# A one-core transformer layer: squares and the sine product on VectorE, softmax rows in pairs, a float32r spread of the norm's factor, and a final norm written in place

## The chip, the cores and the metric

The program runs on one core of a Trainium2 chip. Five engines work on it, each through a queue of its own that it takes strictly in order: TensorE (PE, with its weight loads PEld), VectorE (DVE), ScalarE (ACT), GpSimd (POOL) and SyncE (SP, which here only issues DMAs). The metric is the device time of one execution in microseconds (us), as a median over runs.

## The reference, cut to what matters

One layer on x of 1024 tokens by 1024 channels, everything in float32:

```python
hn = rmsnorm(h, norm_mix)                       # x / sqrt(mean(x*x) + eps) * gain
qa, ka, va, qb, kb, vb = split(hn @ w_in)       # 8 heads / 2 kv heads, and 8 heads, of 64
qa, ka = partial_rope(qa), partial_rope(ka)     # [x1*cos - x2*sin, x2*cos + x1*sin, rest]
o_a = window attention, |i-j| <= 128, with a sink logit in each softmax row
o_b = 2-D neighbourhood attention, 8 x 16 window, with a bias
h = h + concat(rmsnorm(o_a), rmsnorm(o_b)) @ w_out
h = h + (silu(conv(hn @ w_gate) + b) * (hn @ w_up)) @ w_down      # hn = rmsnorm(h, norm_ffn)
return rmsnorm(h, norm_final)
```

## The kernel before, in words

Tensors lie transposed, channels on the 128 partitions and the 1024 tokens along the row, so x is eight tiles of 128x1024. A float32 product is made of three float32r matmuls, high by high, high by low and low by high: each operand is split into a rounded part (`hi`, cast by ACT) and the rest (`lo`, subtracted by DVE). `block` (lines 112 to 115) and `group` (783 to 787) issue the three, each 128x128 by 128x512. PE takes its instructions in the order of the program text (line 91). DVE, ACT, POOL and SP are put in order by a scheduler at build time, from priorities and its own estimate of when things are ready; what it decided is a fixed row of instructions on each engine.

**Start and first norm.** For each of the eight tiles of x, ACT writes `xgh` (line 125) and DVE `xgl` (126), and PE multiplies them at once with the first two weight tiles (`first`, banks `pj` and `o`); the norm's factor is applied only afterwards. Beside it `squares` (135 to 143) squares the tiles on ACT (`sq`, 139) and adds them up, tile after tile, on the engine that its caller names (141): POOL for the first norm (560), DVE for the norm of group A later on. `inverse_narrow` (145) sums the squares over the partitions: 128x1 matmuls with `ones` give a 128x4 column block `ss`, ACT takes the root (153), DVE the reciprocal (154). `widen` (157) spreads that `v` over all partitions again: four float32 matmuls of each 128-column against the identity in `cst` (161), each of which the trace counts as two rows. ACT copies the result into `rstd` (574). This is done for the token halves h = 0 and 1; then `evacuate` (168, line 170) multiplies the banks `pj`, `o` and `s` (third weight tile) with `rstd` on DVE.

**Projections and attention.** Sixteen more projections follow, mixed with attention as filler. `rotate` (178 to 185) applies the rotary part to a tile `t` of heads: two small DMAs fetch the partner channels into `u`, DVE makes t*rc (183), POOL u*rs (184), DVE adds (185). `split_pair` (188) then scales and splits the tile into the operands `q` (190, 192) and moves halves by DMA. Scores (266) come into banks `s`; `softmax` (277 to 290) runs per row block j: POOL copies the sink logit beside it (283), DVE adds the mask and takes the row maximum in one custom instruction (284, with a small read of the result `nm`), ACT the exponential with its sum `sm` (288), DVE the reciprocal of `sm` (289), POOL scales the block (290). Two blocks share a tile `p`; PE transposes them (322, 395), ACT and DVE split the result (`ph`, `pl`, 295 and 296), PE multiplies by v (327, 328).

**Feed-forward and end.** The gated feed-forward runs as matrix products p1 to p7 over blocks, then the down-projection (banks `dn`, order written out at 1049 to 1057) as seven products p. `leave` (1202) adds each finished 128x512 bank to the residual (`add`, 1176) and squares it (`square`, 1180; DVE adds to the running sum at 1185). When p = 6 has begun, the token half h = 1 is complete: `inverse_narrow` for it at (j, c) = (0, 2) and `finish` at (1, 2), while PE goes on with `dn`. The half h = 0 is finished after the last matmul (1245). `finish` (1188) widens v, lets ACT copy the bank into `wide` (1191), and makes eight output tiles: for d = 2 and 5 ACT scales the residual (1196) and POOL multiplies by the copy (1197), for the other six DVE does both in one instruction that reads the bank (1199). They go to `y` tiles, of a pool tag with six buffers, and SP sends them out in the order of d (1200).

## Time and profile before

| | |
|---|---|
| median of 3 runs | 1141.33 us (1141.04 to 1143.16) |
| profiled execution: time / span | 1136.96 / 1135.0 us |
| PE busy / mean granted clock | 1088.1 us (96% of the span) / 0.986 |
| DVE, ACT, POOL busy | 874.7, 550.2, 149.1 us |
| chain that ended last | PE 82%, DVE 8%, DMA 3%, issue 3%, ACT 2%, POOL 1% |

The rows of the timeline view read: start, duration, engine, line, operation, output tile <- input tiles, shape, count, and in brackets the idle time of that engine before it with what ended it. Rows of several like instructions are joined (x4). A window row gives, for a stretch of time, its length and then the busy time (and count) of PE, PEld, DVE, ACT and POOL, the granted PE clock, the busy share of the DMA engines and GB/s. A matmul row lasts longer than the step to the next one, since they are pipelined: at full clock one 128x512 matmul starts 0.23 us after the one before it.

### The profile page before, as it was taken

The numbers are of one execution on the slowest core, as the hardware profiler recorded it, in microseconds if no ns is written. First come the engines' busy times: TensorE is split into PE (matmuls) and PEld (weight loads), VectorE is DVE, ScalarE is ACT, GpSimd is POOL, SyncE is SP. The second block draws the span as 40 slices with busy tenths as digits, with TensorE's granted clock in tenths as the row PEclk, the third lists the DMA queues.
The fourth block names the chain that finished last, engine by engine and source line by source line (L and its number), as shares of the span: only waits on it lengthen the run. The fifth ranks groups of instructions, "written<-read, shape, count | busy, mean of one in ns | idle before, by whom it ended". The sixth has DMA issues, their size and how long they took to land.

```text
span 1135.0 us, 15044 instructions
## 1 busy us (share of the span) xinstructions
PE 1088.1 (96%) x5124; PEld 903.0 (80%) x5124; DVE 874.7 (77%) x1594; ACT 550.2 (48%) x1033; POOL 149.1 (13%) x233
## 2 busy tenths in 40 slices
PE   7989999999999989999899999999999899999995
PEld 5867788888878878888688888888888688888884
DVE  6687888766689667899988778877887778886843
ACT  6235677655767534445443334333433554543531
POOL 4634533233223100000000000000000000000001
PEclk8999999999999999999999999999999999999998
DMA  7242120233305317402542223222322799775723
GB/s 273 72 119 74 48 57 28 73 95 89 78 28 150 101 47 241 146 31 96 192 131 103 107 89 129 94 103 93 123 101 93 232 319 298 260 226 163 261 78 148
DMA packets 65294, 147.17 MB, mean 130 GB/s; under 512 B 7969, under 2 KB 14113, under 8 KB 65217
## 3 DMA queue, kind: packets, MB, share of 16 engines
q1 hardware_dynamic: 56256, 121.17, 34.1%
q10 hardware_dynamic: 8960, 25.04, 5.8%
q8 instruction: 40, 0.66, 0.2%
q14 instruction: 38, 0.30, 0.1%
HBM read 104.37 MB, written 28.57 MB: 117 GB/s over the span
## 4 chain that ended last, share of the span: by engine, by line
PE 82%; DVE 8%; DMA 3%; issue 3%; ACT 2%; POOL 1%; SPq 0%; POOLq 0%; ACTq 0%; DVEq 0%
PE dn L785 6%; PE dn L786 6%; PE dn L787 6%; PE pj L113 6%; PE pj L114 6%; PE pj L115 6%; PE z L785 5%; PE z L787 5%; PE z L786 5%; PE x L785 3%; PE x L786 3%; PE x L787 3%; PE y L787 3%; PE y L785 3%; PE y L786 3%; PE s L266 3%
## 5 line engine op out<-in xcount | busy, mean ns | idle before, releaser
L774 ACT ACTIVATE whi<-ws 128x512 fp32r<-128x512 f32 (+1 forms) x100 | 60.1, 623 | 125.4 <-DVE ws L891 85.5
L785 PE MATMUL dn<-xd,whi 128*128 128x512 f32 x308 | 120.0, 390 | 0.0
L787 PE MATMUL dn<-xd,wlo 128*128 128x512 f32 x308 | 119.8, 389 | 0.0
L786 PE MATMUL dn<-xd,whi 128*128 128x512 f32 x308 | 119.8, 389 | 0.0
L785 PE MATMUL z<-hg,whi 128*128 128x512 f32 x264 | 103.4, 392 | 2.4 <-DVE gs L941 2.4
L787 PE MATMUL z<-hg,wlo 128*128 128x512 f32 x264 | 103.7, 393 | 0.2 <-DVE wlo L775 0.2
L113 PE MATMUL pj<-xgh,whi 128*128 128x512 f32 x248 | 103.8, 418 | 0.0
L786 PE MATMUL z<-hg,whi 128*128 128x512 f32 x264 | 103.3, 391 | 0.0
L290 POOL TENSOR_SCALAR p<-p,sm 128x384 f32<-128x384 f32 (+1 forms) x128 | 77.4, 606 | 192.1 <-DVE sm L289 165.3
L1197 POOL TENSOR_TENSOR y<-y,wide 128x512 f32<-128x512 f32 x4 | 5.1, 1280 | 734.1 <-ACT y L1196 734.1
L288 ACT ACTIVATE p<-p,nm 128x385 f32<-128x385 f32 (+3 forms) x128 | 74.9, 586 | 49.4 <-DVE nm L284 43.9
L114 PE MATMUL pj<-xgl,whi 128*128 128x512 f32 x248 | 97.8, 394 | 0.3 <-DVE xgl L126 0.3
L115 PE MATMUL pj<-xgh,wlo 128*128 128x512 f32 x248 | 98.1, 396 | 0.0
L775 DVE TENSOR_TENSOR wlo<-raw,whi 128x512 fp32r<-128x512 f32 (+1 forms) x102 | 66.5, 671 | 22.1 <-ACT whi L774 21.1
L774 ACT ACTIVATE whi<-raw 128x512 fp32r<-128x512 f32 (+1 forms) x102 | 61.0, 612 | 46.3 <-DMA raw<-in_w_down_dram 11.1
L775 DVE TENSOR_TENSOR wlo<-ws,whi 128x512 fp32r<-128x512 f32 (+1 forms) x100 | 66.9, 681 | 19.8 <-ACT whi L774 19.7
L296 DVE TENSOR_TENSOR pl<-pt,ph 128x384 fp32r<-128x384 f32 (+2 forms) x108 | 63.2, 588 | 21.5 <-ACT ph L295 20.2
L295 ACT ACTIVATE ph<-pt 128x384 fp32r<-128x384 f32 (+2 forms) x108 | 55.3, 514 | 40.6 <-PE pt L395 29.4
L1098 ACT ACTIVATE xd<-xd 128x512 fp32r<-128x512 f32 x77 | 46.9, 626 | 54.1 <-DMA xd<-x 50.7
L787 PE MATMUL y<-hg,wlo 128*128 128x512 f32 x176 | 69.4, 394 | 2.2 <-DVE wlo L775 2.2
L785 PE MATMUL y<-hg,whi 128*128 128x512 f32 x176 | 69.1, 393 | 1.9 <-ACT whi L774 1.9
L785 PE MATMUL x<-hg,whi 128*128 128x512 f32 x176 | 68.8, 391 | 1.4 <-ACT c L925 1.4
(201 smaller groups left out, 2721.9 us busy)
## 6 DMA issues: line engine op xcount, KB each, us to landing
xd<-x SPq DMA_DIRECT2D x77, 256.0 KB, 4.9
raw<-in_w_down_dram SPq DMA_DIRECT2D x72, 256.0 KB, 3.5
raw<-in_w_gate_dram SPq DMA_DIRECT2D x22, 512.0 KB, 3.4
raw<-in_w_up_dram SPq DMA_DIRECT2D x22, 512.0 KB, 5.6
x<-c ACTq DMA_DIRECT2D x22, 512.0 KB, 2.9
raw<-in_w_in_dram SPq DMA_DIRECT2D x32, 256.0 KB, 2.7
raw<-in_w_down_dram SPq DMA_DIRECT2D x36, 192.0 KB, 3.9
x<-t ACTq DMA_DIRECT2D x11, 512.0 KB
```

Source lines behind the costliest of these rows:

```text
L113: nc.tensor.matmul(ps, w[0], x[0][:, tsl(h)], start=first, stop=False)
L114: nc.tensor.matmul(ps, w[0], x[1][:, tsl(h)], start=False, stop=False)
L115: nc.tensor.matmul(ps, w[1], x[0][:, tsl(h)], start=False, stop=last)
L288: nc.scalar.activation(p[:, j, 0:e], p[:, j, 0:e], AF.Exp, bias=nm, scale=-1.0, accum_out=sm)
L290: nc.gpsimd.tensor_scalar(p[:, j, 0:n], p[:, j, 0:n], sm, 1.0, op0=ALU.mult, op1=ALU.mult)
L295: nc.scalar.activation(ph[:, 0:n], ps[:, 0:n], AF.Copy)
L296: nc.vector.tensor_tensor(pl[:, 0:n], ps[:, 0:n], f32(ph[:, 0:n]), op=ALU.subtract)
L774: nc.scalar.activation(hi, src, AF.Copy)
L775: nc.vector.tensor_tensor(lo, src, f32(hi[:, :, :]), op=ALU.subtract)
L785: nc.tensor.matmul(ps, w[0], x[0], start=first and i == 0, stop=False, skip_group_check=True)
L786: nc.tensor.matmul(ps, w[0], x[1], start=False, stop=False, skip_group_check=True)
L787: nc.tensor.matmul(ps, w[1], x[0], start=False, stop=last and i == len(ws) - 1, skip_group_check=True)
```

## The change

Six things change.

1. **Squares:** the first norm's sum of squares is added up by DVE, not POOL.
2. **Sine product:** u*rs of `rotate` moves from POOL to DVE.
3. **Softmax in pairs:** the two blocks of a tile share a 128x2 `sm`; one reciprocal and both POOL scalings follow when the second block is there, and one copy brings both sinks.
4. **Spread in float32r:** `inverse_narrow` splits the factor on DVE (a cast to `v4h`, a subtraction to `v4l`), and `widen` sends both, eight single-pass matmuls against a float32r identity instead of four float32 ones. The sums over partitions run operand by operand, no longer column by column. `ones` shrinks to a column.
5. **End of the final norm:** `finish` widens twice, into one bank for DVE and one for ACT's copy; the outputs are written over the residual tiles, with no `y`; for d = 2 and 5 ACT scales the residual ahead of time (`scaled`, at p = 6), so that only POOL's product remains.
6. **Last tile:** its addition and square go in two halves of 256 columns.

```diff
-        ones = cpool.tile([128, 128], F32, name="ones")
+        ones = cpool.tile([128, 1], F32, name="ones")
...
+        ident_r = cpool.tile([128, 128], F32R, name="ident_r")
...
         def inverse_narrow(sqs, dim, tag):
             ps = bank("ss", tag)
-            for c in range(4):
-                for i, sq in enumerate(sqs):
+            for i, sq in enumerate(sqs):
+                for c in range(4):
                     nc.tensor.matmul(ps[:, c:c + 1], sq[:, c * 128:(c + 1) * 128], ones[:, 0:1], start=c == 0 and i == 0,
                                      stop=i == len(sqs) - 1, skip_group_check=True)
             v = cpool.tile([128, 4], F32, name="v4", tag="v4", bufs=4)
+            hi, lo = (cpool.tile([128, 4], F32R, name=n, tag=n, bufs=4) for n in ("v4h", "v4l"))
             nc.scalar.activation(v, ps[:, 0:4], AF.Sqrt, bias=eps, scale=float(D) / dim)
             nc.vector.reciprocal(v, v)
-            return v
+            nc.vector.tensor_copy(hi, v)
+            nc.vector.tensor_tensor(lo, v, f32(hi[:, :]), op=ALU.subtract)
+            return hi, lo
...
             for c in range(4):
-                nc.tensor.matmul(wide[:, c * 128:(c + 1) * 128], v[:, c:c + 1].to_broadcast([128, 128]), ident, start=True, stop=True)
+                for i, part in enumerate(v):
+                    nc.tensor.matmul(wide[:, c * 128:(c + 1) * 128], part[:, c:c + 1].to_broadcast([128, 128]), ident_r,
+                                     start=c == 0 and i == 0, stop=i == 1, skip_group_check=True)
...
-            nc.gpsimd.tensor_tensor(u[0:n], u[0:n], rs[0:n], op=ALU.mult)
+            nc.vector.tensor_tensor(u[0:n], u[0:n], rs[0:n], op=ALU.mult)
...
-        def softmax(p, j, ps, n, bias, nsink=None):
+        def softmax(st, j, ps, n, bias, nsink=None):
...
+                if j == 0:
+                    st["sm"], st["n"] = spool.tile([128, 2], F32, name="sm"), [n, n]
+                sm, st["n"][j] = st["sm"], n
+                if nsink is not None and j == 0:
+                    nc.gpsimd.tensor_copy(p[:, 0:2, n:n + 1], nsink.rearrange("p (j o) -> p j o", o=1))
...
-                nc.vector.reciprocal(sm, sm)
-                nc.gpsimd.tensor_scalar(p[:, j, 0:n], p[:, j, 0:n], sm, 1.0, op0=ALU.mult, op1=ALU.mult)
+                if j == 1:
+                    nc.vector.reciprocal(sm, sm)
+                    for i, m in enumerate(st["n"]):
+                        nc.gpsimd.tensor_scalar(p[:, i, 0:m], p[:, i, 0:m], sm[:, i:i + 1], 1.0, op0=ALU.mult, op1=ALU.mult)
...
+        nc.gpsimd.tensor_copy(ident_r, ident)
...
-        acc = squares(xts, nc.gpsimd)
+        acc = squares(xts, nc.vector)
...
         def finish(h, v, tag):
             wide = widen(v, tag)
             copy = half("wide")
-            nc.scalar.activation(copy, wide, AF.Copy)
+            nc.scalar.activation(copy, widen(v, tag), AF.Copy)
             for d in range(KT):
-                y = half("y")
                 x = res[d][:, tsl(h)]
-                if d % 3 == 2:
-                    nc.scalar.activation(y, x, AF.Copy, scale=col(C_NFIN + d))
-                    nc.gpsimd.tensor_tensor(y, y, copy, op=ALU.mult)
+                if d in (2, 5):
+                    nc.gpsimd.tensor_tensor(x, x, copy, op=ALU.mult)
                 else:
-                    nc.vector.scalar_tensor_tensor(y, x, col(C_NFIN + d), wide, op0=ALU.mult, op1=ALU.mult)
-                nc.sync.dma_start(out[d, :, tsl(h)], y)
+                    nc.vector.scalar_tensor_tensor(x, x, col(C_NFIN + d), wide, op0=ALU.mult, op1=ALU.mult)
+                nc.sync.dma_start(out[d, :, tsl(h)], x)
+        def scaled(d, h):
+            x = res[d][:, tsl(h)]
+            nc.scalar.activation(x, x, AF.Copy, scale=col(C_NFIN + d))
...
+                if (d, h) == (KT - 1, 0):
+                    s2 = half("s2")
+                    for cols in (slice(0, 256), slice(256, HALF)):
+                        add(d, h, ps, cols)
+                        nc.scalar.activation(s2[:, cols], res[d][:, cols], AF.Square)
+                    sq[h] = [sq[h], s2]
+                    return
...
+            if p == 6 and (j, c) in ((0, 1), (3, 1)):
+                for d in (2, 5):
+                    scaled(d, 1 if j == 0 else 0)
```

How the rows on the engines move is shown at three places. The first is VectorE's row at the start, from the second tile of x to the weight parts `wlo` that follow the first norm. Before:

```order
L126 SCALAR_TENSOR_TENSOR xgl<-xt,par,xgh 128x1024 x2
L109 TENSOR_TENSOR wlo<-raw,whi 128x512
L126 SCALAR_TENSOR_TENSOR xgl<-xt,par,xgh 128x1024 x3
L109 TENSOR_TENSOR wlo<-raw,whi 128x512
L126 SCALAR_TENSOR_TENSOR xgl<-xt,par,xgh 128x1024 x2
L542 TENSOR_SCALAR nsink<-par 128x8
L566 TENSOR_TENSOR wlo_314<-raw_312,whi_313 128x1024
```

and with the change (L127 is the old L126, L142 the old L141, L110 the old L109):

```order
L127 SCALAR_TENSOR_TENSOR xgl<-xt,par,xgh 128x1024
L142 TENSOR_TENSOR sq<-sq 128x1024
L127 SCALAR_TENSOR_TENSOR xgl<-xt,par,xgh 128x1024
L110 TENSOR_TENSOR wlo<-raw,whi 128x512
L142 TENSOR_TENSOR sq<-sq 128x1024
L127 SCALAR_TENSOR_TENSOR xgl<-xt,par,xgh 128x1024
L142 TENSOR_TENSOR sq<-sq 128x1024
L127 SCALAR_TENSOR_TENSOR xgl<-xt,par,xgh 128x1024 x2
L110 TENSOR_TENSOR wlo<-raw,whi 128x512
L127 SCALAR_TENSOR_TENSOR xgl<-xt,par,xgh 128x1024
L142 TENSOR_TENSOR sq<-sq 128x1024
L556 TENSOR_SCALAR nsink<-par 128x8
```

The seven additions of squares now stand between the `xgl`; three of them ahead of the fourth `xgl`, and the last three behind the seventh, ahead of `wlo` of the third weight tile.

The second place is VectorE's row where the first norm's factor is made and the first banks are multiplied by it (`rstd` of half 0 first, then half 1). Before:

```order
L154 RECIPROCAL v_351<-v_351 128x4
L170 TENSOR_TENSOR t<-pj,rstd_345 128x512
L154 RECIPROCAL v_365<-v_365 128x4
L170 TENSOR_TENSOR t<-o,rstd_345 128x512
L170 TENSOR_TENSOR t<-s,rstd_345 128x512
L170 TENSOR_TENSOR t<-pj,rstd_345 128x512
```

and with the change:

```order
L157 RECIPROCAL v_353<-v_353 128x4
L158 CAST v4h<-v_353 128x4
L159 TENSOR_TENSOR v4l<-v_353,v4h 128x4
L177 TENSOR_TENSOR t<-pj,rstd_347 128x512
L157 RECIPROCAL v_375<-v_375 128x4
L177 TENSOR_TENSOR t<-o,rstd_347 128x512
L158 CAST v4h<-v_375 128x4
L177 TENSOR_TENSOR t<-s,rstd_347 128x512
L159 TENSOR_TENSOR v4l<-v_375,v4h 128x4
L177 TENSOR_TENSOR t<-pj,rstd_347 128x512
```

The cast and the subtraction of half 0 follow its reciprocal at once; those of half 1 stand behind the multiplications of the banks `o` and `s`.

The third place is VectorE's row where the first four score blocks of attention come (L284, now L295; `nm` is the read of the maximum), beside the 64-row rotation of a key tile (L183 and L185, now L190 to L192). Before:

```order
L183 TENSOR_TENSOR t<-t,rc 64x1024
L284 ISA p,nm<-s,cst,nsink 128x256
L284 ISA nm 128x1
L284 ISA p,nm<-s,cst,nsink 128x256
L284 ISA nm 128x1
L185 TENSOR_TENSOR t<-t,u 64x1024
L284 ISA p,nm<-s,cst,nsink 128x256
L284 ISA nm 128x1
L289 RECIPROCAL sm<-sm 128x1
```

and with the change:

```order
L295 ISA p,nm<-s,cst,nsink 128x256
L295 ISA nm 128x1
L295 ISA p,nm<-s,cst,nsink 128x256
L295 ISA nm 128x1
L190 TENSOR_TENSOR t<-t,rc 64x1024
L191 TENSOR_TENSOR u<-u,rs 64x1024
L301 RECIPROCAL sm<-sm 128x2
L192 TENSOR_TENSOR t<-t,u 64x1024
L295 ISA p,nm<-s,cst,nsink 128x256
```

The first two score blocks now stand ahead of the whole rotation, and the third stands behind it, three 64x1024 instructions and a reciprocal later than the second. At the end of the program SP's outputs, eight for each half, leave as d = 0, 1, 3, 2, 4, 5, 6, 7; before they left as 0 to 7.

23 lines of the change are left out of this document (10 added, 13 removed).

## The prediction

> **What bounds the kernel now.** The first view is the page's busy time by engine, the second the table of windows (length, then busy time of PE, PEld, DVE, ACT and POOL, granted clock, DMA share, GB/s).
>
> ```profile
> PE 1088.1 (96%) x5124; PEld 903.0 (80%) x5124; DVE 874.7 (77%) x1594; ACT 550.2 (48%) x1033; POOL 149.1 (13%) x233
> ```
>
> ```profile
> 0.00:45.00 45.00, 37.13 (x149) 28.76 (x150) 29.99 (x21) 25.11 (x31) 27.44 (x31) 0.92 0.58 200
> 45.00:80.00 35.00, 30.19 (x153) 25.15 (x152) 28.28 (x39) 11.24 (x21) 13.64 (x8) 0.99 0.40 103
> 80.00:160.00 80.00, 74.56 (x387) 61.84 (x387) 64.69 (x189) 50.89 (x128) 34.55 (x73) 0.98 0.20 53
> 160.00:400.00 240.00, 235.17 (x1281) 199.76 (x1280) 181.23 (x487) 152.20 (x353) 68.30 (x117) 1.00 0.30 82
> 565.00:880.00 315.00, 315.00 (x1391) 260.84 (x1390) 251.60 (x354) 123.73 (x186) 0.00 (x0) 1.00 0.31 107
> 1100.00:1135.00 35.00, 22.70 (x114) 19.05 (x112) 11.98 (x18) 6.02 (x10) 5.12 (x4) 0.84 0.32 121
> ```
>
> PE is the bound, and in the middle it is never idle (315.00 of 315.00). No edit takes a matmul away there, so the change can only win where PE waits: about 8 us in the first window, 5 in each of the next two, 5 in the fourth, and 12 in the last, most of it behind PE's last matmul. I go through these stages and follow in each what PE waits for.
>
> **Start: squares off POOL.** PE's timeline has three waits in the first projections, all for DVE.
>
> ```profile
> 20.51 0.39 PE L113 MATMUL pj<-xgh,w 128*128 128x512 f32 x1
> 22.44 0.50 PE L114 MATMUL pj<-xgl,w 128*128 128x512 f32 x1 [1.54 <-DVE xgl L126]
> 25.77 0.50 PE L114 MATMUL pj<-xgl,whi 128*128 128x512 f32 x1 [0.32 <-DVE xgl L126]
> 27.57 0.51 PE L115 MATMUL o<-xgh,wlo 128*128 128x512 f32 x1 [0.58 <-DVE wlo L109]
> ```
>
> A row lasts 0.39 where the steps are 0.23, so each wait costs its bracket plus 0.16: 1.54 + 0.32 + 0.58 + 3 x 0.16 = 2.9 us; each of the three matmuls is also 0.11 longer than the row at 20.51. Together 3.3 us. Why is DVE late? The groups of lines 126 and 141 give shortest, median and longest duration in ns, and two rows of the timeline show one meeting:
>
> ```profile
> L126 DVE SCALAR_TENSOR_TENSOR xgl<-xt,par,xgh x7: 1270/2627/3422, 11.6 to 30.8; 128x1024 fp32r<-128x1024 f32 x7
> L141 POOL TENSOR_TENSOR sq<-sq x7: 2382/2722/3262, 12.6 to 37.0; 128x1024 f32<-128x1024 f32 x7
> L141 DVE TENSOR_TENSOR sq<-sq x3: 1215/1226/1228, 285.5 to 290.5; 128x1024 f32<-128x1024 f32 x3
> ```
>
> ```profile
> 27.12 2.65 POOL L141 TENSOR_TENSOR sq<-sq 128x1024 f32<-128x1024 f32 x1 [2.49 <-ACT sq L139]
> 27.44 4.62 DVE L126 SCALAR_TENSOR_TENSOR xgl<-xt,par,xgh 128x1024 fp32r<-128x1024 f32 x2
> ```
>
> An `xgl` alone takes 1.27; up to 3.42 where POOL adds squares. The pair at 27.44 lasts 4.62, not 2.5: its first sits until POOL ends at 29.77 and then needs its own 1.1, its second is short. So the slow rows are waits for POOL. With the additions on DVE at 1.22 each, seven cost 8.5 us, and the slow rows give back about as much or more. What counts is when each `xgl` is due. By the new order, the fourth `xgl` (the one PE waits for at 22.44) has ahead of it two others, `wlo` and two additions, all at 1.2 or less, from 11.6 on: it is ready near 18.4, and PE wants it at 20.74. The last addition ends near 31.5 by the same count, where POOL's last began at 37.0. I take **-3.3**. The ends are -3.3 and, with the slow rows left as they are and 8.5 us more on DVE, +8.
>
> **First spread.** DVE's rows from the second reciprocal on, and PE's second spread:
>
> ```profile
> 46.93 0.17 DVE L154 RECIPROCAL v<-v 128x4 f32<-128x4 f32 x1
> 47.01 0.66 DVE L170 TENSOR_TENSOR t<-o,rstd 128x512 f32<-128x512 f32 x1
> 47.59 0.68 DVE L170 TENSOR_TENSOR t<-s,rstd 128x512 f32<-128x512 f32 x1
> ```
>
> The cast and the subtraction on 128x4 aren't in the trace; the nearest row is this reciprocal, 0.17, so 0.25 for both as they overlap (ends 0.15 and 0.4). For half 1 they also stand behind `o` and `s`: 0.66 + 0.68 + 0.25 is 1.6 us more before PE can spread, and the third tile's second half is queued behind that spread on PE. Both this and the rotation below run into a wait that PE has anyway:
>
> ```profile
> 52.99 5.79 POOL L184 TENSOR_TENSOR u<-u,rs 64x1024 f32<-64x1024 f32 x2 [5.01 <-DMA u<-t]
> 56.47 3.40 DVE L185 TENSOR_TENSOR t<-t,u 64x1024 f32<-64x1024 f32 x1 [1.05 <-POOL u L184]
> 62.13 1.21 DVE L185 TENSOR_TENSOR t<-t,u 128x1024 f32<-128x1024 f32 x1
> 77.66 0.36 PE L266 MATMUL s<-ka,q 128*128 128x256 f32 x1 [3.33 <-DMA q<-t]
> 78.72 0.44 PE L266 MATMUL s<-ka,q 128*128 128x384 f32 x1 [0.35 <-DVE nm L284]
> ```
>
> PE waits 3.33 for the first `q`. Its chain gains the 1.05 that DVE waited for POOL, 3.40 - 1.21 = 2.2 in that addition and about 1 in a later one that meets POOL; it pays 1.6 and three products at 1.2. That is between 0.5 earlier and 0.8 later; near zero, so the 1.6 and the products are covered by these gains. What is late next is the fifth score (78.72), which needs its bank emptied by the third `p,nm`. In the new order the whole rotation of the key tile, three instructions at 1.2, stands between the second and the third: the first scores stand just ahead of PE's wait, which began 3.33 before 77.66, so the two first can run from 75.0 to 76.0, the rotation to 79.4, so the fifth score comes near 79.9, **+1.2** against the shifted frame (ends 0, if the rotation meets idle time, and 2.4, if `q` is late as well).
>
> **Attention.** After that, POOL's product is gone from where it hurt:
>
> ```profile
> 115.58 3.46 POOL L184 TENSOR_TENSOR u<-u,rs 128x1024 f32<-128x1024 f32 x1
> 121.47 0.50 PE L328 MATMUL o<-pl,v 128*128 128x512 f32 x1 [1.41 <-DVE pl L296]
> 125.82 0.50 PE L328 MATMUL o<-pl,v 128*128 128x512 f32 x1 [1.03 <-DVE pl L296]
> L322 PE MATMUL pt<-cst,p 128*128 128x128 f32 x176 | 26.6, 273 | 0.2 <-POOL p L290 0.2
> POOL p L290 <- DVE sm L289: 165.3, 89, 6.2
> DVE sm L289 <- ACT p L288: 15.0, 32, 0.8
> ```
>
> The product held up the scalings of `p`, and with them the transposes and `pl`: the two waits are worth 1.41 + 1.03 + 2 x 0.16 = 2.8. Against that DVE gets two products of 1.2 in a window where it is busy 64.69 of 80. Pairing takes away 64 reciprocals and part of the 15.0 us in which DVE stood at one of them, and holds the first block's scaling back by an exponential, 0.6; POOL waited 165.3 us for DVE in all, so it has the time, and the transposes come later by program. I take **-1** (ends -3.1 and +2.3), and 0 for 160 to 1100, where PE waits for little (ends -0.5 and +0.5).
>
> The Trainium skill, "SBUF — State Buffer", section "Who interferes with whom", speaks against the products here: a VectorE instruction with two SBUF inputs and a GpSimd instruction that reads SBUF exclude each other, and the later one waits in full. The rows at 27.12 and 27.44 agree. By it each new product could meet a scaling of `p` and add 0.6; two of them make this term +0.2 and the sum -3.7.
>
> **End.** First the half 1 in the middle of `dn`, then the rows behind the last `dn`, and the first output's step in the chain:
>
> ```profile
> 1103.26 1.05 PE L161 MATMUL sw<-cst,v 128*128 128x128 f32 x8
> 1119.35 0.69 DVE L1176 TENSOR_TENSOR h<-dn,h 128x512 f32<-128x512 f32 x1 [5.33 <-PE dn L787]
> 1120.08 0.63 ACT L1180 ACTIVATE s<-h 128x512 f32<-128x512 f32 x1 [6.78 <-DVE h L1176]
> 1120.76 1.72 PE L150 MATMUL ss<-ones,s 128*128 128x1 f32 x14 [1.33 <-ACT s L1180]
> 1123.05 1.55 PE L161 MATMUL sw<-cst,v 128*128 128x128 f32 x8 [0.57 <-DVE v L154]
> 1124.68 0.60 ACT L1191 ACTIVATE wide<-sw 128x512 f32<-128x512 f32 x1 [1.90 <-PE sw L161]
> 1125.31 2.72 DVE L1199 SCALAR_TENSOR_TENSOR y<-h,par,sw 128x512 f32<-128x512 f32 x4 [2.32 <-ACT wide L1191]
> 1130.42 0.75 DVE L1199 SCALAR_TENSOR_TENSOR y<-h,par,sw 128x512 f32<-128x512 f32 x1 [0.78 <-POOL y L1197]
> ```
>
> ```profile
> 1126.09 2.08 DMA out_dram<-y
> ```
>
> A float32 spread is eight rows at 0.11 us, and the float32r one also has eight; I price it the same (ends 0.5 and 1.1 for a spread). The second spread for half 1 goes straight into PE's row: **+0.9**. At the very end: the halves let the first square start before the second addition, -0.2; behind the last square stand 4 of the 14 rows, 10 x 0.12 less, -1.1 with what their order costs; cast and subtraction +0.25; the spread at the pace of 1103 instead of 1123, -0.65, since PE has less of a pause before it; DVE no longer stands behind ACT's copy, -0.6. DVE's outputs start at 1123.1 instead of 1125.3. From there eight outputs at one per 0.69 (DVE's row: 2.72 for four) and the 2.08 of a transfer end near 1130.8; before, the last output was only begun at 1130.42, behind POOL's second product, which by the same 2.08 lands at 1133.3 at the earliest. ACT's copy comes 0.9 later than it could, behind the second spread, and POOL's products near 1125.7 and 1127.0, in time for their places in SP's row. I take **-2.7** (ends -1.8 and -3.2).
>
> The Trainium skill, "TensorE: Matmul & The Clock Gate", Part 1, says that TensorE's clock halves after an idle window of about 3.4 us that runs free of the kernel. The 1.55 here beside 1.05 at 1103 agrees. By it the pause still decides at this place, and if the spread stays slow the end gives -2.0 and the sum is -4.2.
>
> **Sum.** -3.3 + 1.2 - 1 + 0.9 - 2.7 = -4.9 us. The profiled execution took 1136.96 (span 1135.0 and 1.96 around it), so it would take 1132.1. The runs' median, 1141.33, lies 4.4 above it; I carry that over and predict **1136.4**.
>
> **Rivals.**
> - *More comes through.* The rotation meets idle time (0 instead of +1.2), PE's clock does not fall after the wait at 77.66 (the window below grants half, so half of 2.3 is lost), and attention gives -2: -3.3 - 1.2 - 2 + 0.9 - 2.7 = -8.3, 1133.0. For it: DVE is idle 7 of 35 us from 45 to 80. Against: the new order of the third place.
>
> ```profile
> 80.00:82.30 2.30, 2.30 (x7) 1.84 (x7) 1.97 (x8) 0.89 (x4) 1.27 (x1) 0.50 0.52 114
> ```
>
> - *Only the end counts.* DVE, with 2.4 us of new products and the order of the third place, makes its successors late: -3.3 + 1.2 + 2.1 + 0.9 - 2.7 = -1.8, 1139.5. For it: both waits at 121 and 125 are put down to DVE. Against: they follow POOL's 3.46.
> - *Slower: the start does not get its relief.* If the long `xgl` rows come of something other than POOL, such as the transfers (DMA share 0.58 in the window), DVE has 8.5 us more in the stage in which PE waits for it: +8 + 1.2 - 1 + 0.9 - 2.7 = +6.4, 1147.7. The other terms make -1.6, so the program is slower once the start costs PE over 1.6, and by a measurable amount from 3.9 on. Against it: the second row of the pair at 27.44 is short as soon as POOL is done.
> - *The pairs wait.* Every `p` scaled 0.6 later on PE's path would cost 64 x 0.6; 8 of them cancel the sum. PE's transposes (L322) waited 0.2 us for `p` in all, and it goes with the slower cases.
>
> **How the numbers follow.** Forecast 0.49; more comes through 0.20; only the end 0.17; slower, both cases, 0.14. About 0.2%, 2.3 us, is what a measurement of this kernel can tell from no change: faster 0.69, same 0.17, slower 0.14. Range: the low ends, -3.3 + 0 - 3.1 - 0.5 + 0.9 - 3.2, and the clock's 1.2, make -10.4, 1130.9; the high ends, without the slow start, -3.3 + 2.4 + 2.3 + 0.5 + 0.9 - 1.8, make +1.0, 1142.3. I give 1130.5 to 1142.3; it leaves out the slower cases.
>
> **What would show it.** Start: `xgl` rows all near 1.3 and no PE wait for `xgl` near 20 to 28. First spread: the spread of half 1 later by 1.6 against half 0. Third place: the fifth score behind the rotation. Attention: no PE wait over 1 us at 119 to 126. End: two spreads of eight, DVE's first output 2.2 us sooner after the last `dn`, outputs landing 0.7 apart. It is wrong if `xgl` rows stay at 2 to 3 us, if waits for `nm` or `pl` grow, or if the last output ends no sooner after the last `dn`.

## The result, and the profile after

| | before | changed |
|---|---|---|
| median over 22 runs each | 1141.13 us (1137.45 to 1143.28) | 1139.35 us (1136.79 to 1142.19) |
| profiled execution, span | 1136.96, 1135.0 | 1140.56, 1138.8 |
| mean granted TensorE clock of that execution | 0.986 | 0.978 |

The ratio is 0.9985, interval 0.9975 to 0.9994: 1.7 us faster (0.7 to 2.8), where 4.9 was forecast. The two profiled executions say the opposite, the changed one is 3.6 us longer. The one of before is quicker than all 22 of its kernel's runs here, the one of the change is among the slower of its own. So times come from the runs below, and the traces serve for single steps, each against its own neighbours.

The page of the changed kernel, busy time and granted clock in 40 slices:

```profile
PE 1096.2 (96%) x5140; PEld 912.6 (80%) x5140; DVE 866.7 (76%) x1564; ACT 549.8 (48%) x1034; POOL 111.4 (10%) x189
...
PEclk8899999999999999999899999999999999999998
```

Its windows (length, busy time of PE, PEld, DVE, ACT, POOL, then granted clock, DMA share, GB/s):

```profile
0.00:45.00 45.00, 39.07 (x160) 31.70 (x160) 25.70 (x31) 25.60 (x33) 11.21 (x20) 0.90 0.58 207
45.00:80.00 35.00, 30.02 (x131) 24.90 (x131) 25.72 (x37) 8.98 (x16) 0.52 (x1) 0.88 0.38 94
80.00:160.00 80.00, 74.95 (x382) 62.93 (x383) 63.43 (x171) 50.79 (x127) 27.81 (x54) 0.96 0.20 53
...
```

From 45 to 80 us PE is busy as long as before, 30.02 against 30.19, and does less: 131 matmuls of all sizes against 153. The clock column says why, 0.88 against 0.99. That is where the gain of the start went.

The start itself came as forecast. Line 126 is now 127; its group (shortest, median, longest in ns):

```profile
L127 DVE SCALAR_TENSOR_TENSOR xgl<-xt,par,xgh x7: 1279/1283/1285, 11.9 to 27.5; 128x1024 fp32r<-128x1024 f32 x7
```

All seven rows last 1.28, none is stretched, and PE has no wait from 20 to 28 us any more. Then come the spreads. PE's timeline before:

```profile
42.90 0.95 PE L150 MATMUL ss<-ones,sq 128*128 128x1 f32 x8
44.46 1.13 PE L161 MATMUL sw<-cst,v 128*128 128x128 f32 x8 [0.61 <-PE ss L150]
...
47.15 1.16 PE L161 MATMUL sw<-cst,v 128*128 128x128 f32 x8 [0.78 <-DVE v L154]
...
54.52 0.39 PE L113 MATMUL pj<-xgh,whi 128*128 128x512 f32 x1
```

and that of the changed kernel:

```profile
40.38 0.95 PE L152 MATMUL ss<-ones,sq 128*128 128x1 f32 x8
42.19 0.30 PE L167 MATMUL sw<-ident_r,v4h 128*128 128x128 f32 x1 [0.86 <-DVE v4h L158]
...
46.25 0.44 PE L167 MATMUL sw<-ident_r,v4h 128*128 128x128 f32 x1 [1.31 <-DVE v4h L158]
46.82 0.48 PE L167 MATMUL sw<-ident_r,v4l 128*128 128x128 f32 x1
...
50.62 0.63 PE L116 MATMUL s<-xgh,wlo 128*128 128x512 f32 x1
...
57.12 0.39 PE L114 MATMUL pj<-xgh,whi 128*128 128x512 f32 x1
...
79.95 0.36 PE L273 MATMUL s<-ka,q 128*128 128x256 f32 x1 [3.61 <-DMA q<-t]
81.01 0.69 PE L273 MATMUL s<-ka,q 128*128 128x384 f32 x1 [0.35 <-DVE nm L295]
```

The first sum over partitions starts at 40.38, where it started at 42.90: 2.5 us ahead. The next projection, whose first matmul (`pj`) follows the third tile's second half, starts at 57.12, where it started at 54.52: 2.6 us behind. The first score that waits for a `q` starts at 79.95, where it started at 77.66: 2.3 us behind. So the lead is lost between the first sum and the next projection. There lie a wait of 0.86 where 0.61 was, a wait of 1.31 for `v4h` where 0.78 was, another step for `v4l`, and matmuls that take 0.63 a row, the slow clock. The windows show when the clock falls:

```profile
40.00:44.00 4.00, 3.14 (x24) 3.01 (x22) 0.51 (x3) 0.86 (x2) 1.29 (x2) 0.89 0.32 90
44.00:46.00 2.00, 0.94 (x5) 0.85 (x4) 1.42 (x4) 0.26 (x1) 0.34 (x1) 0.50 0.08 22
46.00:48.00 2.00, 1.62 (x7) 1.47 (x7) 0.77 (x4) 0.00 (x0) 0.00 (x0) 0.50 0.38 103
```

In narrower windows it is at one half from 43.1 to 53.3 us. It falls ahead of the wait of 1.31, which begins at 44.9; what stands before the fall is the first sum and the wait of 0.86. DVE's timeline shows the queue in front of `v4l`:

```profile
45.27 0.18 DVE L157 RECIPROCAL v<-v 128x4 f32<-128x4 f32 x1 [0.58 <-ACT v L156]
45.37 0.66 DVE L177 TENSOR_TENSOR t<-o,rstd 128x512 f32<-128x512 f32 x1
45.95 0.16 DVE L158 CAST v4h<-v 128x4 fp32r<-128x4 f32 x1
46.01 0.69 DVE L177 TENSOR_TENSOR t<-s,rstd 128x512 f32<-128x512 f32 x1
46.61 0.15 DVE L159 TENSOR_TENSOR v4l<-v,v4h 128x4 fp32r<-128x4 f32 x1
```

The cast and the subtraction take 0.31 together and are done 1.5 after the reciprocal began, since each stands behind a bank multiplication, as the rows in the section on the change have it.

The last `dn` of the kernel before, and then the end of the changed kernel, PE, DVE, ACT, POOL and SP from the last `dn` on:

```profile
1118.92 0.39 PE L787 MATMUL dn<-xd,wlo 128*128 128x512 f32 x1
```

```profile
1124.24 0.39 PE L801 MATMUL dn<-xd,wlo 128*128 128x512 f32 x1
...
1124.66 0.76 DVE L1191 TENSOR_TENSOR h<-dn,h 128x256 f32<-128x256 f32 x2 [5.39 <-PE dn L801]
1125.12 0.75 ACT L1228 ACTIVATE s<-h 128x256 f32<-128x256 f32 x2 [6.58 <-DVE h L1191]
1125.59 1.05 PE L152 MATMUL ss<-ones,s 128*128 128x1 f32 x8 [0.18 <-ACT s L1228]
...
1128.64 4.04 DVE L1209 SCALAR_TENSOR_TENSOR h<-h,par,sw 128x512 f32<-128x512 f32 x6 [1.09 <-PE sw L167]
...
1129.42 5.63 SPq L1210 DMA_DIRECT2D out_dram<-h  x8
...
1130.29 0.60 ACT L1203 ACTIVATE wide<-sw 128x512 f32<-128x512 f32 x1 [3.35 <-PE sw L167]
1130.97 2.49 POOL L1207 TENSOR_TENSOR h<-h,wide 128x512 f32<-128x512 f32 x2 [18.11 <-ACT wide L1203]
```

DVE's first output starts 4.4 us after the last `dn` (before: 6.4) and its six run without a hole. The span ends 14.5 after the last `dn`, before it was 16.0.

### The profile page after: what moved, and what is told of

It is laid out like the page before. It is cut to its first block, busy times and chain, and to the rows that moved or that the text cites. A ratio compares the mean times of both kernels' runs of the same rounds, so it can differ in the third digit from the quotient of the medians.

```text
span 1138.8 us, 14934 instructions
## 1 busy us (share of the span) xinstructions
PE 1096.2 (96%) x5140; PEld 912.6 (80%) x5140; DVE 866.7 (76%) x1564; ACT 549.8 (48%) x1034; POOL 111.4 (10%) x189
## 4 chain that ended last, share of the span: by engine, by line
PE 74%; DVE 9%; issue 3%; ACT 2%; DMA 1%; POOL 1%; POOLq 0%; ACTq 0%; DVEq 0%
PE pj L114 6%; PE pj L115 6%; PE pj L116 6%; PE dn L799 6%; PE dn L800 6%; PE dn L801 6%; PE z L799 4%; PE z L800 4%; PE z L801 4%; PE x L799 3%; PE x L800 3%; PE x L801 3%; PE y L801 3%; PE y L799 3%; PE y L800 3%; PE s L273 3%
## 5 line engine op out<-in xcount | busy, mean ns | idle before, releaser
L789 DVE TENSOR_TENSOR wlo<-raw,whi 128x512 fp32r<-128x512 f32 (+1 forms) x102 | 66.7, 672 | 22.5 <-ACT whi L788 22.2
L1207 POOL TENSOR_TENSOR h<-h,wide 128x512 f32<-128x512 f32 x4 | 5.0, 1282 | 735.1 <-ACT wide L1203 735.1
```

The lines of the kernel that those rows point to most:

```text
L789: nc.vector.tensor_tensor(lo, src, f32(hi[:, :, :]), op=ALU.subtract)
```

## The experiments

The changed kernel's loss at the spread gave the first theories; they are named in the expectations. A: the start wins what was forecast, and the queue ahead of the second spread together with a slower clock behind it takes it back. B: the sine products and the pairs on DVE take it back, and the wait for the first `q` covers the spread. C: the sine products cost within the change what they cost alone. D: the loss is spread over the program by chance of the clock. Ratios are against runs of the kernel before on the same chip, with 95% intervals; in us they are ratio times 1140. Differences "to the change" subtract its -1.7, and carry both intervals, so they are good to about 2 us. Each kernel ran 5 to 12 times, and left one trace.

| run | ratio (interval) | us to before | clock, 40 to 56 us | first sum to next projection | first sum to first q | end behind last dn |
|---|---|---|---|---|---|---|
| before (trace) | 1 | 0 | 1.00 | 11.6 | 34.8 | 16.0 |
| changed | 0.9985 (0.9975 to 0.9994) | -1.7 | 0.68 | 16.7 | 39.6 | 14.5 |
| e1 squares only | 0.9970 (0.9956 to 0.9985) | -3.4 | 1.00 | 11.6 | 35.2 | 17.1 |
| e2 sine only | 1.0026 (1.0009 to 1.0042) | +3.0 | 1.00 | 11.6 | 34.4 | 16.2 |
| e3 pairs only | 1.0012 (0.9997 to 1.0027) | +1.4 | 0.79 | 14.5 | 36.3 | 16.7 |
| e4 spread and end | 1.0015 (1.0003 to 1.0028) | +1.7 | 0.79 | 15.7 | 37.4 | 15.0 |
| f1 split on POOL | 1.0003 (0.9991 to 1.0015) | +0.3 | 0.79 | 17.1 | 40.0 | 14.1 |
| f2 pause filled | 0.9968 (0.9954 to 0.9983) | -3.6 | 1.00 | 9.9 | 35.0 | 15.4 |
| f3 sine on POOL | 0.9978 (0.9960 to 0.9996) | -2.5 | 0.68 | 16.8 | 39.0 | 15.4 |
| f4 one spread, half 1 | 0.9967 (0.9951 to 0.9983) | -3.8 | 0.79 | 16.1 | 38.8 | 14.5 |
| g1 old first spread | 0.9948 (0.9931 to 0.9966) | -5.9 | 0.89 | 13.2 | 36.0 | 14.3 |
| g2 filled, one spread, sine on POOL | 0.9999 (0.9988 to 1.0010) | -0.1 | 1.00 | 9.9 | 39.3 | 14.8 |
| g3 filled, one spread | 0.9957 (0.9944 to 0.9970) | -4.9 | 1.00 | 9.9 | 35.0 | 13.8 |
| g4 before, filled | 1.0038 (1.0024 to 1.0053) | +4.3 | 1.00 | 9.9 | 39.7 | 16.1 |
| h1 clock held | 0.9972 (0.9960 to 0.9983) | -3.2 | 0.89 | 14.6 | 37.5 | 15.4 |
| h2 old first spread, one spread | 0.9936 (0.9914 to 0.9957) | -7.3 | 1.00 | 11.6 | 34.5 | 13.9 |
| h3 output order | 0.9991 (0.9979 to 1.0004) | -1.0 | 0.79 | 15.9 | 38.7 | 15.0 |
| h4 old first spread, no pairs | 0.9955 (0.9939 to 0.9972) | -5.1 | 1.00 | 11.6 | 34.4 | 15.3 |

The last four columns come from each run's trace: the granted clock of one window, and then differences in us, from the start of the first `ss` matmul to that of the first `pj` of the next projection (42.90 and 54.52 in the trace of before) and to that of the first score that waits (77.66 there; it waits for `q`, in g4 for `t`), and from the start of the last `dn` matmul to the end of the span. Where the pause is filled (f2, g2, g3, g4), twelve more matmuls of the third tile stand ahead of the spreads.

**e1: the squares alone.**

```diff
-        acc = squares(xts, nc.gpsimd)
+        acc = squares(xts, nc.vector)
```

> The kernel before with one edit: the first norm's sum of squares on VectorE. Theory A (the start wins what was forecast; the queue in front of the second spread's low part and the slower clock behind it take it back; sine product and pairs are neutral): -3.0 us against the kernel before (-2.0 to -4.0), all xgl rows near 1.28, no wait of PE for xgl from 20 to 28, and the lead still there at the first scores. Theory B (the sine products and the pairs on VectorE take the gain back): the same -3.0 here. If the lead is gone at the first scores even without the new spread, both are wrong and the start was covered anyway: -1 to 0.

-3.4 us, and first sum to first `q` is 35.2: the lead of 3.0 at the first sum (39.95 against 42.90) is still 2.5 at `q`. By the middle of the intervals this part alone is worth more than the whole change.

**e2: the sine product alone.**

```diff
-            nc.gpsimd.tensor_tensor(u[0:n], u[0:n], rs[0:n], op=ALU.mult)
+            nc.vector.tensor_tensor(u[0:n], u[0:n], rs[0:n], op=ALU.mult)
```

> The kernel before with one edit: u*rs of the rotation on VectorE. Theory A: between -1.0 and +1.0 us; the chain of the first q gains from rows that no longer meet POOL what three products of 1.2 cost it. Theory B: +1.5 to +3.0, with longer waits of PE for nm and pl between 75 and 130.

+3.0 us, as B had it, but not where B had it: the first `q` is as quick as before (34.4), and PE's waits for `nm` and `pl` from 75 to 130 us are 4.4 in all, as in the trace of before. The mean granted clock of its runs is 0.979 against 0.9825 of before; where they lose it, one trace can't tell. f3 and g3 below speak against a cost of 3.0 within the change.

**e3: the pairs alone** (`softmax` and its two calls as in the change, all else as before).

> The kernel before with one edit: softmax rows in pairs (one sink copy, one reciprocal, both scalings after the second block). Theory A: -0.7 to +0.7 us. Theory B: +0.7 to +2.0, with PE waiting for POOL's p at the transposes.

+1.4 (-0.3 to +3.1): not told from nothing. The sign that B named is missing: PE's transposes never wait for POOL's `p` in its trace. The trace has the slow clock from 46.5 to 53.3 us, in code that is the same as before; so that place is hit now and then without any edit to it.

**e4: the spread and the end alone** (the change without squares, sine product and pairs).

> The change without its squares, sine product and pairs: the float32r spread everywhere, two spreads at the end, outputs in place, the last tile in halves. Theory A: +1.0 to +3.0 us against the kernel before: about +1.7 for the second spread of the first norm queued behind two bank multiplications, 0 to 2 for slower matmul steps behind it, +0.9 for the extra spread at half 1, -1.5 at the end. Theory B: -0.5 to -1.5, the end less the extra spread, since the wait at 47 is covered.

+1.7, with 37.4 from first sum to first `q` and 15.0 at the end: the loss at the spread without the squares' gain. B, which saw -0.5 to -1.5 here, falls. The four parts sum to +2.7, the change gives -1.7: they do not add.

**f1: the split of the first norm's factor on POOL.**

```diff
-        def inverse_narrow(sqs, dim, tag):
+        def inverse_narrow(sqs, dim, tag, eng=nc.vector):
...
-            nc.vector.tensor_copy(hi, v)
-            nc.vector.tensor_tensor(lo, v, f32(hi[:, :]), op=ALU.subtract)
+            eng.tensor_copy(hi, v)
+            eng.tensor_tensor(lo, v, f32(hi[:, :]), op=ALU.subtract)
...
-            return widen(inverse_narrow([sq], dim, tag), tag)
+            return widen(inverse_narrow([sq], dim, tag, nc.gpsimd), tag)
```

> The change with one edit: in the first norm the cast to v4h and the subtraction to v4l run on GpSimd, so that they no longer stand behind bank multiplications on VectorE. Theory A (the second spread's wait is on the path): -1.0 to -2.0 us against the change, -2.5 to -4.0 against the kernel before; PE waits about 0.9 instead of 1.3 and 0.4 ahead of the second spread. Theory B (the wait for the first q covers it): -0.3 to +0.3 against the change.

The edit did not do what it was to do. POOL's timeline, then PE's:

```profile
44.56 0.96 POOL L372 TENSOR_TENSOR xb<-cst,rr 128x384 f32<-128x384 f32 x1 [3.36 <-DMA rr<-in_rpb_dram]
45.48 0.71 POOL L373 TENSOR_TENSOR xb<-cst,rr 128x256 f32<-128x256 f32 x1
46.13 0.19 POOL L158 CAST v4h<-v 128x4 fp32r<-128x4 f32 x1
```

```profile
46.37 0.47 PE L167 MATMUL sw<-ident_r,v4h 128*128 128x128 f32 x1 [3.29 <-POOL v4h L158]
```

The cast now stands behind two bias products that wait for a DMA, and PE waits 3.29 instead of 1.31. Two more us of wait, and the runs are 2.0 slower than the change: the opposite edit to the one meant, and it speaks for A just as well. In the traces the next projection comes 17.1 us after the first sum, and 15.9 and 16.1 in h3 and f4, which had the same clock, 0.79: 1.0 to 1.2 of the 2.0 arrive there, and 1.2 to 1.3 at the first `q`. The wait isn't covered.

**f2: PE's pause filled.**

```diff
-        for h in range(2):
-            nc.scalar.activation(rstd1[:, tsl(h)], inverse_rms_wide(acc[:, tsl(h)], D, "pt"), AF.Copy)
+        narrow = [inverse_narrow([acc[:, tsl(h)]], D, "pt") for h in range(2)]
+        rest_of = enumerate(product(ps3[1], third.w, xg, 1))
+        for _ in range(4):
+            next(rest_of)
+        for h in range(2):
+            nc.scalar.activation(rstd1[:, tsl(h)], widen(narrow[h], "pt"), AF.Copy)
...
-        for i, _ in enumerate(product(ps3[1], third.w, xg, 1)):
-            if i == 3:
+        for i, _ in rest_of:
+            if i == 6:
                 first[0].post()
-            if i == 6:
+            if i == 7:
                 first[1].post()
```

> The change with one edit in PE's order: both sums over partitions first, then twelve matmuls of the third tile's second half, then both spreads, then the other twelve. PE no longer pauses while the factor is made. Theory A: -2.0 to -5.0 us against the change: the two pauses, 2.5 in all, and the slower clock behind them go, less what the first banks get later. Theory B: -1.0 to 0 against the change, the wait for the first q grows by what the pauses lose.

-3.6, 1.9 better than the change: just short of A's -2.0, and nearer to it than to B's. The wait for the first `q` does grow, from 3.61 to 5.09, but that `q` comes 4.6 sooner after the first sum (35.0 and 39.6). The window from 40 to 56 us in the changed kernel, and then in this one:

```profile
40.00:56.00 16.00, 13.70 (x63) 11.87 (x62) 5.43 (x14) 2.49 (x6) 1.63 (x2) 0.68 0.16 46
```

```profile
40.00:56.00 16.00, 16.00 (x87) 13.70 (x87) 11.61 (x19) 3.18 (x6) 1.66 (x2) 1.00 0.12 35
```

Filled, PE starts 87 matmuls there instead of 63, at full clock.

**f3: the sine product back on POOL**, as the `-` line of e2 in the changed kernel.

> The change with one part undone: u*rs of the rotation back on GpSimd. Theory A (the product is neutral where the squares have left GpSimd): -1.0 to +1.0 us against the change. Theory C (the products on VectorE cost what they cost alone, +3.0): -2.0 to -3.0 against the change, with shorter waits of PE for pl between 95 and 130.

0.8 better than the change: within A's range, though the uncertainty reaches C's -2. In the traces the product on POOL brings the first `q` 22.2 us after the next projection's start, on VectorE 22.8 (changed); against that, its attention is dearer, as told below.

**f4: one spread at half 1.**

```diff
-            nc.scalar.activation(copy, widen(v, tag), AF.Copy)
+            nc.scalar.activation(copy, widen(v, tag) if h == 0 else wide, AF.Copy)
```

> The change with one edit: at half 1 ScalarE's copy is taken from the first spread, and the second spread of that half is left out; half 0 keeps both. If the extra spread is in PE's row: -0.9 us against the change, and the dn matmuls behind it start 0.9 sooner. If it hides behind something: 0.

-2.1 to the change, more than the 0.9, and inside its uncertainty. In the traces the step is clean: against the trace of before, the changed kernel loses 0.89 at half 1 (its `dn` matmuls move from 4.42 behind to 5.31), and this one loses nothing there.

**g1: the old spread in the first norm only.** `inverse_rms_wide` returns to the four float32 matmuls on `v`, without cast and subtraction:

```diff
-        def inverse_narrow(sqs, dim, tag):
+        def inverse_narrow(sqs, dim, tag, split=True):
...
+            if not split:
+                return v
...
-            return widen(inverse_narrow([sq], dim, tag), tag)
+            v = inverse_narrow([sq], dim, tag, False)
+            wide = bank("sw", tag)
+            for c in range(4):
+                nc.tensor.matmul(wide[:, c * 128:(c + 1) * 128], v[:, c:c + 1].to_broadcast([128, 128]), ident, start=True, stop=True)
+            return wide
```

> The change with one part undone at one place: the first norm's factor is spread by the four float32 matmuls of before, with no cast and no subtraction; all else as changed. Theory A (the new spread's wait at 43 to 47 and the slower clock behind it cost about 2): -1.5 to -3.0 us against the change, so about -3.3 to -4.8 against the kernel before, and a granted clock near 1.00 from 40 to 56 us. Theory D (the loss is spread over the program, by chance of the clock): -0.5 to +0.5 against the change.

-5.9, that is -4.2 to the change (about 2 either way): more than A's -1.5 to -3.0 by the middle value, and D falls. The clock from 40 to 56 us is 0.89 in its trace, not near 1.00 as A had it; h2 and h4, with the same spread, have 1.00. With this one step undone, the time is 1.0 from the forecast.

**g2 and g3: filled pause and one spread at half 1, with the sine product on POOL (g2) and on DVE (g3).**

> The change with three edits: PE's pauses in the first norm filled as before (sums, twelve matmuls, spreads, twelve matmuls), one spread at half 1, the sine product back on GpSimd. If the gains add: -1.9 - 0.9 and -0.8 for the sine, -3.5 us against the change, -5.2 against the kernel before. If the wait for the first q takes back what is filled: -1.5 against the change.

> As the one before, but with the sine product on VectorE as in the change: -1.9 - 0.9 = -2.8 us against the change, -4.5 against the kernel before. If the products on VectorE cost what they cost alone (+3.0), it stands 2 to 3 behind the run with the product on GpSimd; if they are neutral where the squares have left GpSimd, the two are within 1.

-0.1 and -4.9. For g3 the gains add (-4.5 was expected), for g2 they do not. No expectation for their difference holds: with the pause filled, POOL's product is the one that costs, 4.8. PE's row in g2 and DVE's rows ahead of it:

```profile
65.52 0.50 PE L114 MATMUL pj<-xgh,whi 128*128 128x512 f32 x1 [4.81 <-DVE t L177]
```

```profile
55.23 3.40 DVE L192 TENSOR_TENSOR t<-t,u 64x1024 f32<-64x1024 f32 x1 [2.29 <-POOL u L191]
58.56 1.21 DVE L190 TENSOR_TENSOR t<-t,rc 128x1024 f32<-128x1024 f32 x1
59.76 1.22 DVE L223 TENSOR_TENSOR kb<-t,ka 64x1024 fp32r<-64x1024 f32 x1
60.90 1.21 DVE L192 TENSOR_TENSOR t<-t,u 128x1024 f32<-128x1024 f32 x1
62.03 2.83 DVE L110 TENSOR_TENSOR wlo<-raw,whi 128x512 fp32r<-128x512 f32 x1
64.79 1.27 DVE L177 TENSOR_TENSOR t<-pj,rstd 128x512 f32<-128x512 f32 x2
```

The third tile's banks come earlier, PE wants the next `pj` earlier, and its emptying (L177) stands behind an addition that waits 2.29 for POOL's `u` and then lasts 3.40, and behind a weight subtraction (L110) that lasts 2.83 beside POOL's next product. With the product on DVE (g3) the same rows take 1.2 and 0.7, and PE's wait there is 0.42.

**g4: the kernel before with the pause filled.**

> The kernel before with PE's order filled in the same way, nothing else. Theory A: the pauses of before, 0.6 and 0.8, are shorter and seldom lower the clock: -0.5 to -1.5 us against the kernel before. If filling is worth the same without the new spread: -2 to -3.

+4.3, where both expectations had a gain: PE's timeline has the same wait for `pj` behind POOL's product as g2. In these four kernels filling the pause helped only where DVE could take the banks.

```profile
68.65 0.79 PE L113 MATMUL pj<-xgh,whi 128*128 128x512 f32 x1 [5.13 <-DVE t L170]
```

**h1: the wait kept, the clock held.** Idle matmuls behind each root of the first norm, three for half 0 and six for half 1:

```diff
-        def inverse_narrow(sqs, dim, tag):
+        def inverse_narrow(sqs, dim, tag, hold=0):
...
             nc.scalar.activation(v, ps[:, 0:4], AF.Sqrt, bias=eps, scale=float(D) / dim)
+            for _ in range(hold):
+                nc.tensor.matmul(ps[:, 128:256], ident, ident, start=True, stop=True, skip_group_check=True)
...
-            nc.scalar.activation(rstd1[:, tsl(h)], inverse_rms_wide(acc[:, tsl(h)], D, "pt"), AF.Copy)
+            nc.scalar.activation(rstd1[:, tsl(h)], widen(inverse_narrow([acc[:, tsl(h)]], D, "pt", 3 + 3 * h), "pt"), AF.Copy)
```

> The change with idle matmuls (identity by identity, into unused columns of the bank ss) in the two pauses of the first norm: three behind the first root, six behind the second. The spreads still wait for the cast and the subtraction as in the change, and come up to 0.5 later; only TensorE is busier meanwhile. If the slower clock behind the pause is most of what is lost there: -1.5 to -2.5 us against the change, granted clock near 1.00 from 40 to 56 us. If the wait itself is most of it: 0 to +0.5 against the change.

-1.5 to the change, at the edge of what can be told, with PE's row and the window:

```profile
43.10 2.63 PE L158 MATMUL ss<-cst 128*128 128x128 f32 x12 [0.35 <-ACT v L156]
```

```profile
40.00:56.00 16.00, 15.51 (x86) 13.96 (x87) 8.92 (x18) 2.37 (x7) 1.64 (x2) 0.89 0.12 32
```

The slow stretch shrinks (clock 0.89, not 0.68) and does not go, so this run does not part the wait from the clock as it was meant to. First sum to first `q` is 37.5: about 2 of the 4.8 us by which the changed kernel's trace is behind the one of before are gone. How the loss divides is read from all traces together, below.

**h2: old first spread and one spread at half 1**, g1 and f4 together.

> The change with the old float32 spread in the first norm and one spread at half 1. If the two add: -4.2 - 0.9, about -5 us against the change and -6.8 against the kernel before, near 1133.5. If the extra spread at half 1 is worth nothing: as with the old first spread alone, -5.9 against the kernel before.

-7.3 (-9.8 to -4.9), near 1132.7 us, faster than both kernels: this is the version that the runs point to. PE's first spreads in it:

```profile
38.64 0.95 PE L152 MATMUL ss<-ones,sq 128*128 128x1 f32 x8
40.20 1.13 PE L177 MATMUL sw<-cst,v 128*128 128x128 f32 x8 [0.61 <-PE ss L152]
41.16 0.95 PE L152 MATMUL ss<-ones,sq 128*128 128x1 f32 x8
42.83 1.16 PE L177 MATMUL sw<-cst,v 128*128 128x128 f32 x8 [0.71 <-DVE v L157]
```

Waits of 0.61 and 0.71, and the lead of 4.3 at 38.64 against before is 4.5 at the first `q`.

**h3: the order of the outputs.**

```diff
-            for d in range(KT):
+            for d in (0, 1, 3, 4, 2, 6, 5, 7):
```

> The change with the outputs of both halves sent as d = 0, 1, 3, 4, 2, 6, 5, 7, so that SyncE does not stand before d = 2 while GpSimd makes it. If this stand is what the end lacks against its forecast: the last output lands 0.7 to 1.2 sooner behind the last dn, -0.7 to -1.2 us against the change. If the transfers' own pace sets the end: 0.

+0.7 to the change, inside the uncertainty. With the spreads at the same slow step as in f3, its end is 15.0 behind the last `dn`, there 15.4; but e4 and h4, in the old order and at nearly the same step, have 15.0 and 15.3. SP's stand before d = 2 is worth 0.4 at most, not the 1.2 that the end of the changed kernel's trace lacks against its forecast.

**h4: old first spread, rows one by one** (g1 with `softmax` as before).

> The change with the old float32 spread in the first norm and the softmax rows one by one as before. If pairing is neutral: within 1.0 us of the run with the old first spread and pairs (-5.9 against the kernel before). If pairs cost what they cost alone, 1.4: -7.3 against the kernel before. If they gain where POOL is relieved: -4 to -5.

-5.1 against -5.9 with pairs, a difference inside the uncertainty: neutral within the change as far as the runs tell.

## Why the prediction was wrong, point by point

- **Start, -3.3: right.** From PE's first matmul on the third tile of x to the first sum, every kernel with the squares on DVE gains 2.8 to 3.4 us against the trace of before, all `xgl` rows are 1.28 or 1.29, and e1 gives -3.4 in time. Collision with POOL was the cause; the rival in which the long rows had another one falls.
- **First spread: the step that failed.** The prediction put 1.6 us of queue in front of the second spread, found about 4.2 of gains on the chain of the first `q` and said "so the 1.6 and the products are covered by these gains". By its own figures the costs, 1.6 and three products at 1.2, were 5.2, about 1 above the gains, and it took the balance as nothing. The products are covered: in the nine traces with the product on VectorE and no filled pause (changed, e2, f1, f4, g1, h1 to h4) the first `q` comes 22.7 to 22.9 us after the start of the next projection, in the trace of before 23.1. The spread is not covered. Those 22.7 to 22.9 stay the same whether the next projection starts 11.6 us after the first sum or 17.1, so what is late at the spread is late at `q`, in full. With the new spread, no filled pause and no held clock (changed, e4, f1, f3, f4, h3) first sum to first `q` takes 37.4 to 40.0 us, with the old spread in the old order (before, e1, e2, e3, g1, h2, h4) 34.4 to 36.3. Undoing the spread is worth 4.2 in time (g1 against the change; 3.5 in h2 against f4, which differ in it alone).

  Two things were missed. The chain of `q` starts from the banks that this very spread releases, so a late spread moves the chain with it, and the gains lie behind it. And the granted clock falls: from 40 to 56 us it is 0.68 to 0.79 in those six traces, and 1.00 in five of the seven with the old spread (0.89 in g1, 0.79 in e3). The way from the first sum to the next projection parts the two. With the old spread it takes 11.6 us at clock 1.00, 13.2 at 0.89 and 14.5 at 0.79; with the new one 14.6 at 0.89 (h1), 15.7 to 16.1 at 0.79 (e4, f4, h3) and 16.7 to 16.8 at 0.68 (changed, f3). At the same clock the new spread is 1.2 to 1.6 later, which is near the 1.6 that the prediction had; the rest, 3.5 or more of the 5.1 that the changed kernel's trace loses there, goes with the clock, a term that the prediction put at nothing here. It had the price of a pause in its own rows, at 74 and at the end, and did not ask for it.
- **Third place, +1.2: wrong, 0.** The rotation does stand before the third `p,nm`, but that one needs the score that waits for `q`, and the rotation ends (80.56) as this score is done: the fifth score comes 1.06 behind that `q` (81.01 and 79.95), as it did before (78.72 and 77.66).
- **Attention, -1: about right.** From 90 to 200 us the four traces with the product on VectorE, pairs and no stretch of slow clock there gain 1.4 or so against the trace of before (f1, g1 and h1 -1.4, h2 -1.5); f3 and g2, with the product on POOL and no slow stretch either, gain about 0.5 and 0.2. With a slow stretch, which shows in about half of the traces, there is no gain. The wait for `pl` near 121 stays, 1.81 at 123.70 in the changed kernel:

```profile
123.70 0.50 PE L341 MATMUL o<-pl,v 128*128 128x512 f32 x1 [1.81 <-DVE pl L309]
```

  VectorE has hardly a gap from 118.4 to 123.6 us there, and the product and the addition of a rotation, 1.2 each, stand ahead of that `pl`. The second wait, near 126, goes with the product on VectorE, and stays in f3 and g2 (0.84 and 0.86). In time, pairs and sine product are neutral within the change as far as h4 and f3 tell. Of the meetings with POOL that were weighed, the changed kernel's trace has two, but not of the products: two pairs of scalings of `p` last 2.11 and 2.23 instead of 1.15, beside a multiplication by `rc` and an addition; the six products last 1.21 to 1.22 each.
- **Half 1, +0.9: right,** 0.89 between the traces of before and of the change.
- **End, -2.7: mis-sized.** The order of events is as forecast. Over the traces with the old end the span ends 16.0 to 17.1 behind the last `dn`, with the new one 13.8 to 15.4, -1.7 between the means of 16.4 and 14.7. Where the spreads run at 0.12 us a row it is 13.8 and 13.9 (g3, h2), where all or nearly all of their rows run at 0.21 it is 15.0 to 15.4 (e4, f2, f3, h1, h4). Against the 16.0 in the trace of before, the quick step, which the prediction took, is worth 2.2 to 2.3 and the slow one 0.6 to 1.0; its terms, -2.7 and -2.0, were too large for both.
- **The sum.** With -3.3, 0, -1, +0.9 and -1.7 the change is at -5.1, and the first spread takes about 4 of it back: near the -1.7 measured, within the uncertainty of that 4. The rival "only the end counts" gave -1.8, by another cause: it blamed DVE's new products and the order of the rows; what it needed was the spread.

Open stay: where the sine product alone loses its 3.0 (e2), how the loss at the spread divides between wait and clock in time rather than in single traces, and why the four parts alone do not add up.

## What to carry to other kernels

A delay ahead of a later wait is covered only if the thing waited for does not itself start from what is delayed: follow that chain back past the delay before calling it covered. Price a pause of TensorE twice, by its length and by the slow matmuls behind it, and prefer to give TensorE its next work first, if the engine that empties the banks can keep up. And a profiled execution is one draw: compare steps between neighbours in a trace, and times over many runs.

## What the runs showed of the hardware that was not expected

The clock falls in pieces of one size. In the changed kernel's trace it is at one half from 43.1 to 53.3 us, for 10.2 us, and at full speed around that. From 40 to 56 us the windows of the eighteen kernels show 1.00, 0.89, 0.79 or 0.68 and nothing else: 0, 1.8, 3.4 or 5.1 us of clock lost in 16, steps of about 1.7, which is 3.4 us at half clock; the 10.2 us are three of them. The Trainium skill, "TensorE: Matmul & The Clock Gate", Part 1, gives a free-running window of about 3.4 us at half rate; the steps agree.

The clock falls without a pause of that length. In f3 it falls at 42.0 us, behind 0.95 us of 128x1 sums and a wait of 0.86, and three pieces follow; with waits of 0.61 and 0.71 to 0.78 five traces of seven lose none.

Which pauses lose a piece changes from trace to trace in code that is the same (e3 lost two from 46.5 to 53.3 us, before none). The mean granted clock goes with a run's time: in the 22 runs of the changed kernel the five quickest, 1136.8 to 1137.8 us, have 0.980 or 0.981, the five slowest, 1140.6 to 1142.2, have 0.978 or 0.979. Their mean is 0.9795, that of the kernel before 0.982 over the 109 runs beside the experiments. The kernels with the old first spread and the squares on VectorE have 0.982 or 0.983 (e1, g1, h2, h4), those with the new one and no filled pause or held clock 0.979 to 0.981 (changed, e4, f1, f3, f4, h3). It is not the spread alone: e2 and e3 keep the old one and have 0.979 and 0.981. So the mean clock of the runs gives a first hint of the longer pauses, and the traces have to say where they are.
